# A hybrid attention and recurrence network: weight sums made by accumulating transfers in place of VectorE additions

## The chip, the cores and the metric

The kernel runs on one core of one Trainium2 chip. The time is that of the device, in microseconds, for one execution of the whole network. Before the change the median of three runs is 2181.79 us (2180.43 to 2184.33). The engines are named as the profile names them: PE (TensorE, matrix products), PEld (its weight loads), DVE (VectorE), ACT (ScalarE), POOL (GpSimd) and SP (SyncE, which here only issues transfers).

## The reference

Two layers over 1024 tokens of width 1024. Layer 0 mixes by windowed attention, layer 1 by a gated recurrence; each is followed by an MLP with a squared ReLU. All is float32.

```python
def sqrelu_mlp(h, w_up, w_down):
    return jnp.square(jax.nn.relu(h @ w_up)) @ w_down

def hgrn2_recurrence(h, lower_bound, w_in, g_norm, w_o):
    q, f, i, g = jnp.split(h @ w_in, 4, axis=-1)
    ...

def reference(...):
    for layer in range(DEPTH):
        h = rmsnorm(x, mix_norm[layer])
        if layer % N_MIXERS == 0:
            y = sliding_window_attention(h, ...)
        else:
            y = hgrn2_recurrence(h, ...)
        x = x + y
        h = rmsnorm(x, mlp_norm[layer])
        x = x + sqrelu_mlp(h, mlp_w_up[layer], mlp_w_down[layer])
    return rmsnorm(x, final_norm)
```

The change touches `h @ w_up` of both MLPs and `h @ w_in` of the recurrence.

## The kernel before

**Tiles.** Tokens stand in two halves of 512 (`hf`), features in blocks of 128. Nearly every tile is 128 x 512 float32, 256 KB. A product in full precision is made of three passes over numbers split in a high and a low part: `weight_split` (L402) casts a weight tile to `wh` (on ACT or DVE) and subtracts to get `wl` (on DVE); `split` does the same for activations into `a` tiles; `mm3` (L384) then issues high x high, high x low and low x high.

**Seven products for eight.** The first product of each MLP, and the recurrent projections, take two column blocks of weights (the `first` and the `second`), two halves of the contraction and two halves of the tokens: a 2 x 2 by 2 x 2 block product. It is made in the Winograd form of Strassen's scheme, with seven block products of 12 matmuls each (`product`, L561) in place of eight. `strassen_weights` (L567) makes the weight side: four tiles are loaded into `wr` buffers (five of them), four sums s1 to s4 are made of them on DVE into `m` buffers (seven), and the seven weights 1 to 7 are split. `finish` (L516) makes the activation side, four sums of four tiles each, at the start of each stage. `pair` (L581) is one such product of an MLP: 16 pairs a layer. `two` (L1058) is that of the recurrent projections, called twice for each of eight blocks e; the first call of each kind finds weights 1 and 2 already done by `two_first`. After the products the results are put together: ACT copies a PSUM tile out while later products add into the same tile (`main`, a `q` buffer of PSUM), DVE adds the copies.

**What sets the order.** No instruction is issued where it is written. `Schedule` (L140) records every operation with its engine, an assumed cost and the buffers it uses, and then makes one list by a simulation of its own: an operation is taken when its inputs and its buffer are free, lowest rank first. Buffers of a tag are handed out in the order of first use. Operations inside `strassen_weights` have a `lead` of 100 ranks, so weights are prepared about a pair ahead. A cast may go to ACT or DVE, whichever the plan finds free. A transfer is planned as 650 to 820 ns on SP and 2000 ns more until it has landed. On the chip each engine then takes its instructions strictly in that order and waits for semaphores. Since there are five `wh` and five `wl` buffers, a weight can be split only when the product of the weight five places earlier has ended.

**Line numbers.** Every operation is recorded through `call`, so in the trace all instructions have line L326 (before) or L328 (after); they are told apart by their tiles.

Of the kernel before, what the change touches and what calls it, by code (L numbers as in the profile page):

```python
# [22 lines left out]
TH = T // NH  # L23
FF = 4096
MT = FF // P
EPS = 1e-5
N_PAR = 8 * KT
# [13 lines left out]
BUFS = {"a": 60, "t": 18, "m": 7, "sm": 8, "wr": 5, "wh": 5, "wl": 5, "p": 4, "q": 4}  # L41
# [95 lines left out]
HK = KT // 2  # L137
# [140 lines left out]
class Net:  # L278
    def __init__(self, ctx, tc, io):
        self.nc, self.io = tc.nc, io  # L280
        self.s = Schedule()
        self.n = 0
        self.x = None
        self.pool = ctx.enter_context(tc.tile_pool(name="sb", bufs=1))
        self.pp = ctx.enter_context(tc.tile_pool(name="ps", bufs=1, space=bass.MemoryType.PSUM))
        self.dram = ctx.enter_context(tc.tile_pool(name="dr", bufs=1, space=bass.MemoryType.DRAM))
        nc = self.nc
        self.par = self.const((P, N_PAR))
        self.dma(self.par, io["par"], 4 * P * N_PAR)
# [104 lines left out]
    def gain(self, which, kt):  # L394
        return self.par[:, which * KT + kt : which * KT + kt + 1]

    def raw(self, src):
        r = self.tile("wr", BUFS["wr"], (P, TH), F32)
        self.dma(r, src, 4 * P * TH)
        return r  # L400

# [94 lines left out]
    def gained(self, which, kt, hf):  # L496

        u = self.t()
        self.act(u, self.x[kt][hf], AF.Copy, scale=self.gain(which, kt))
        return u  # L500

    def weigh(self, hf):
# [5 lines left out]
    def begin(self, which):  # L508

        self.b, self.u = {k: [] for k in range(1, 8)}, []  # L510
        for kt in range(KT):
            u = self.gained(which, kt, 0)
            self.b[1 + kt // HK].append(self.split(u))
            self.u.append(self.keep(u))

    def finish(self, which, upper_first=False):  # L516

        x, t, q01, q11 = self.b, [], [], []

        def stored(j):  # L520
            z = self.t()
            self.dma(z, self.u[j], 4 * P * TH)
            return z

        def lower():
            for j in range(HK):
                q01.append(self.gained(which, j, 1))
                t.append(stored(j))
                self.tt("any", t[j], q01[j], t[j], ALU.subtract)
                x[5].append(self.split(t[j]))  # L530

        def upper():
            for j in range(HK):
                q11.append(self.gained(which, j + HK, 1))
                x[3].append(self.split(q11[j]))

        for part in (upper, lower) if upper_first else (lower, upper):
            part()
        for j in range(HK):
            self.tt("any", t[j], q11[j], t[j], ALU.subtract)  # L540
            x[6].append(self.split(t[j]))
        for j in range(HK):
            self.tt("any", q01[j], q11[j], q01[j], ALU.subtract)
# [23 lines left out]
    def strassen_weights(self, first, second, done=()):  # L567

        self.s.lead = LEAD
        a = {(i, k): self.raw(src[:, k * TH : k * TH + TH]) for i, src in enumerate((first, second)) for k in range(2)}  # L570
        s1, s2, s3, s4 = (self.t(tag="m") for _ in range(4))
        self.tt("any", s1, a[1, 0], a[1, 1], ALU.add)
        self.tt("any", s2, s1, a[0, 0], ALU.subtract)
        self.tt("any", s3, a[0, 0], a[1, 0], ALU.subtract)
        self.tt("any", s4, a[0, 1], s2, ALU.subtract)
        order = ((1, a[0, 0]), (5, s1), (2, a[0, 1]), (6, s2), (3, s4), (7, s3), (4, a[1, 1]))
        w = {name: self.weight_split(z) for name, z in order if name not in done}
        self.s.lead = 0
        return w

# [477 lines left out]
    def two(self, which, e, x, out, begun=None):  # L1058

        w = self.strassen_weights(*(self.io["win"][i, e] for i in which), (1, 2) if begun else ())  # L1060
        main, y0 = begun or (self.psum(), self.t())
        side, own = self.psum(), begun or self.psum()
        y1, z0, z1 = (self.t() for _ in range(3))
        out += [(y0, y1), (z0, z1)]
        if not begun:
            self.product(main, w[1], x[1], True)
            self.copy(y0, main)
# [5 lines left out]
        self.copy(y1, main)  # L1073
        yield
        if not begun:
            self.product(own, w[2], x[2], True)
            self.tt("DVE", y0, own, y0, ALU.add)
# [5 lines left out]
        self.tt("DVE", y1, side, y1, ALU.add)  # L1083
        yield
        self.product(main, w[4], x[4], False)
        self.copy(z0, main)
        yield
# [287 lines left out]
```

## Time and profile before

| | before |
|---|---|
| median of 3 runs | 2181.79 us |
| span of the profiled execution, first to last instruction | 2174.9 us |
| granted clock of PE, mean over the span | 0.994 |
| DMA moved | 316.49 MB, 44.7% of the 16 engines' span |
| chain that ended last: PE, DVE, ACT, DMA | 85%, 7%, 4%, 2% |

Of the profiled execution the record has the span, and no time of its own beside it. The stages in the span: attention until about 295 us, first MLP `pair` loop 295 to 600, its second product until 935, recurrent stage 935 to 1455, its output product until 1510, second MLP 1510 to 2150, final norm at the end. A row of a group has the instruction, output and input tiles, shapes, count, then busy time and mean of one, then the idle time of the engine just ahead of such instructions and what ended it. In a row of the timeline the first number is the start in us from the span's start and the second how long it took; what stands in brackets is the idle time ahead of it and its releaser. In a row of the windows each engine has its busy time and, in parentheses, its instructions.

### The profile page before, as it was taken

The numbers are of one execution on the slowest core, as the hardware profiler recorded it, in microseconds if no ns is written. First come the engines' busy times: TensorE is split into PE (matmuls) and PEld (weight loads), VectorE is DVE, ScalarE is ACT, GpSimd is POOL, SyncE is SP. The second block draws the span as 40 slices with busy tenths as digits, with TensorE's granted clock in tenths as the row PEclk, the third lists the DMA queues.
The fourth block names the chain that finished last, engine by engine and source line by source line (L and its number), as shares of the span: only waits on it lengthen the run. The fifth ranks groups of instructions, "written<-read, shape, count | busy, mean of one in ns | idle before, by whom it ended". The sixth has DMA issues, their size and how long they took to land.

```text
span 2174.9 us, 32278 instructions
## 1 busy us (share of the span) xinstructions
PE 2129.5 (98%) x11374; PEld 1713.3 (79%) x11374; DVE 1823.6 (84%) x3608; ACT 837.7 (39%) x1757; POOL 62.4 (3%) x124
## 2 busy tenths in 40 slices
PE   8999999999999999999999999999999999999997
PEld 6777778888877887877788888878788887888786
DVE  8899889667789888899888888878976678988887
ACT  5567755122234233365333333343521223322442
POOL 4030000000000000000100000000000000000000
PEclk9999999999999999999999999999999999999999
DMA  6212363333369867741111111547333336976652
GB/s 204 75 48 83 112 194 116 105 109 111 108 204 305 274 202 234 247 136 49 56 57 59 58 53 52 188 148 227 113 114 103 107 116 224 305 241 226 209 171 78
DMA packets 174274, 316.49 MB, mean 146 GB/s; under 512 B 19616, under 2 KB 21664, under 8 KB 174112
## 3 DMA queue, kind: packets, MB, share of 16 engines
q1 hardware_dynamic: 174112, 314.43, 44.7%
q8 instruction: 89, 1.46, 0.3%
q14 instruction: 73, 0.60, 0.1%
HBM read 250.39 MB, written 63.96 MB: 145 GB/s over the span
## 4 chain that ended last, share of the span: by engine, by line
PE 85%; DVE 7%; ACT 4%; DMA 2%; issue 1%; SPq 0%; DVEq 0%; ACTq 0%
PE q L326 45%; PE p L326 40%; DVE a L326 3%; DVE t L326 2%; ACT t L326 1%; ACT a L326 1%; DVE wl L326 1%; DVE m L326 1%; DMA wr<-in_down 1%; ACT m L326 1%; ACT wh L326 0%; DMA t<-d 0%; DVE wh L326 0%; DMA d<-t 0%; DMA a<-d 0%
## 5 line engine op out<-in xcount | busy, mean ns | idle before, releaser
L326 PE MATMUL q<-a,wh 128*128 128x512 f32 x2560 | 798.6, 395 | 5.0 <-DVE t L326 2.3
L326 PE MATMUL p<-a,wh 128*128 128x512 f32 x2336 | 754.4, 402 | 9.1 <-ACT t L326 3.7
L326 PEld LDWEIGHTS q<-a,wh 128*128 128x128 f32 x2560 | 480.1, 188 | 120.5 <-ACT t L326 4.1
L326 PEld LDWEIGHTS p<-a,wh 128*128 128x128 f32 x2336 | 432.0, 189 | 107.7 <-ACT t L326 4.6
L326 PE MATMUL q<-a,wl 128*128 128x512 f32 x1280 | 499.5, 394 | 0.0
L326 PE MATMUL p<-a,wl 128*128 128x512 f32 x1168 | 462.8, 397 | 0.0
L326 PEld LDWEIGHTS q<-a,wl 128*128 128x128 f32 x1280 | 240.4, 188 | 56.6
L326 PEld LDWEIGHTS p<-a,wl 128*128 128x128 f32 x1168 | 220.4, 189 | 50.5 <-issue 0.5
L326 DVE TENSOR_TENSOR wl<-wr,wh 128x512 fp32r<-128x512 f32 x352 | 241.0, 686 | 15.5 <-ACT wh L326 5.4
L326 ACT COPY t<-q 128x512 f32<-128x512 f32 (+2 forms) x201 | 111.8, 562 | 349.0 <-PE q L326 344.1
L326 DVE TENSOR_TENSOR a<-t,a 128x512 fp32r<-128x512 f32 (+1 forms) x294 | 195.0, 685 | 0.8 <-DMA t<-d 0.5
L326 DVE CAST wh<-wr 128x512 fp32r<-128x512 f32 x204 | 87.8, 430 | 127.6 <-PE p L326 78.4
L326 DVE TENSOR_TENSOR wl<-m,wh 128x512 fp32r<-128x512 f32 x256 | 176.3, 689 | 16.1 <-ACT wh L326 6.1
L326 ACT CAST wh<-m 128x512 fp32r<-128x512 f32 x153 | 95.2, 623 | 210.4 <-PE q L326 148.4
L326 DVE TENSOR_TENSOR t<-t,t 128x512 f32<-128x512 f32 (+3 forms) x268 | 159.7, 611 | 17.7 <-DMA t<-d 10.7
L326 ACT CAST a<-t 128x512 fp32r<-128x512 f32 x189 | 114.7, 619 | 128.8 <-PE q L326 82.6
L326 ACT CAST wh<-wr 128x512 fp32r<-128x512 f32 x148 | 91.1, 619 | 172.7 <-PE p L326 109.3
L326 PE MATMUL p<-wh,a 128*128 128x512 f32 x384 | 130.6, 407 | 8.2 <-ACT a L326 7.0
L326 DVE TENSOR_TENSOR m<-wr,wr 128x512 f32<-128x512 f32 x160 | 109.7, 687 | 22.2 <-DMA wr<-in_down 11.9
L326 PEld LDWEIGHTS q<-t,t 128*64 128x64 f32 (+1 forms) x2160 | 98.0, 144 | 25.0 <-issue 11.2
L326 PE MATMUL q<-t,t 128*64 128x32 f32 (+2 forms) x2160 | 111.5, 230 | 0.0
L326 DVE CAST wh<-m 128x512 fp32r<-128x512 f32 x103 | 44.3, 430 | 73.4 <-PE q L326 59.7
(117 smaller groups left out, 2113.9 us busy)
## 6 DMA issues: line engine op xcount, KB each, us to landing
t<-d SPq DMA_DIRECT2D x296, 256.0 KB, 4.7
wr<-in_down SPq DMA_DIRECT2D x256, 256.0 KB, 3.9
d<-t SPq DMA_DIRECT2D x180, 256.0 KB, 2.4
wr<-in_up SPq DMA_DIRECT2D x128, 256.0 KB, 2.9
wr<-in_win SPq DMA_DIRECT2D x68, 256.0 KB, 2.9
a<-d SPq DMA_DIRECT2D x60, 256.0 KB, 4.4
wr<-in_wqkv SPq DMA_DIRECT2D x48, 256.0 KB, 2.8
d<-a SPq DMA_DIRECT2D x48, 256.0 KB, 2.4
```

The costliest lines, as they stand in the source:

```text
L326: fn(*[place(a) for a in args], **{k: place(v) for k, v in kw.items()})
```

## The change

The four sums of `strassen_weights` are no longer made by DVE. Two `m` tiles are loaded by SP, `rows` with A10 and `column` with A00, and further tiles are added to them in place by transfers that POOL issues with an accumulate operation (`accumulate`): `rows` becomes A10 + A11 (weight 5), then + A00 (weight 6), then + A01 (weight 3); `column` is A00 (weight 1), then + A10 (weight 7). Between two additions to a tile its split has to be done. Weights 2 and 4 are loaded by themselves. So a pair has four loads on SP as before, and four accumulating transfers besides, and uses two `m` buffers in place of four, two `wr` in place of four.

Sums with only plus signs need other signs elsewhere: the first half's activations are scaled by the negative gain (`neg_par`, one new constant), several differences in `finish` become sums or one `scalar_tensor_tensor`, `two` copies products out with a scale of -1, and in `pair` the lower half of the hidden rows, which now has the opposite sign, is squared with `min` in place of `max`. The plan assumes 1100 ns on POOL and 2500 ns more for an accumulating transfer.

```diff
+        self.neg_par = self.const((P, N_PAR))
+        self.ts("DVE", self.neg_par, self.par, -1.0, None, ALU.mult, None, N_PAR)
...
+    def accumulate(self, out, in_, nbytes):
+
+        self.op("Pool", self.nc.gpsimd.dma_start, [out], [in_, out], 1100.0, out, in_, accum_op=ALU.add, tail=2500.0)
...
-        if psum:
+        if m < MT // 2:
+            self.stt(r, c, 0.0, c, ALU.min, ALU.mult)
+        elif psum:
...
-                self.tt("any", t[j], q01[j], t[j], ALU.subtract)
+                self.tt("any", t[j], q01[j], t[j], ALU.add)
...
-            self.tt("any", t[j], q11[j], t[j], ALU.subtract)
+            self.stt(t[j], q11[j], -1.0, t[j], ALU.mult, ALU.subtract)
...
-            self.tt("any", z, z, t[j], ALU.subtract)
+            self.stt(z, z, -1.0, t[j], ALU.mult, ALU.subtract)
...
-        a = {(i, k): self.raw(src[:, k * TH : k * TH + TH]) for i, src in enumerate((first, second)) for k in range(2)}
-        s1, s2, s3, s4 = (self.t(tag="m") for _ in range(4))
-        self.tt("any", s1, a[1, 0], a[1, 1], ALU.add)
-        self.tt("any", s2, s1, a[0, 0], ALU.subtract)
-        self.tt("any", s3, a[0, 0], a[1, 0], ALU.subtract)
-        self.tt("any", s4, a[0, 1], s2, ALU.subtract)
-        order = ((1, a[0, 0]), (5, s1), (2, a[0, 1]), (6, s2), (3, s4), (7, s3), (4, a[1, 1]))
-        w = {name: self.weight_split(z) for name, z in order if name not in done}
+        a = {(i, k): src[:, k * TH : k * TH + TH] for i, src in enumerate((first, second)) for k in range(2)}
+        rows, column = self.raw(a[1, 0], "m"), self.raw(a[0, 0], "m")
+        self.accumulate(rows, a[1, 1], 4 * P * TH)
+        w = {}
+
+        def made(name, z):
+            if name not in done:
+                w[name] = self.weight_split(z)
+
+        made(1, column)
+        made(5, rows)
+        if 2 not in done:
+            made(2, self.raw(a[0, 1]))
+        self.accumulate(rows, a[0, 0], 4 * P * TH)
+        made(6, rows)
+        self.accumulate(rows, a[0, 1], 4 * P * TH)
+        made(3, rows)
+        self.accumulate(column, a[1, 0], 4 * P * TH)
+        made(7, column)
+        made(4, self.raw(a[1, 1]))
...
-        self.copy(y0, main)
+        self.act(y0, main, AF.Copy, scale=-1.0)
...
-            self.tt("DVE", y0, own, y0, ALU.add)
+            self.tt("DVE", y0, y0, own, ALU.subtract)
```

DVE's queue in the steady `pair` loop, before: from the split of weight 1 to that of weight 6, and on to the last sums. `m1164` is the tile of weight 5, `m1165` that of weight 6; the `m12..` tiles are sums for the next pair.

```order
CAST wh1170_4680<-m1164_4585 128x512
TENSOR_TENSOR wl1171_4686<-m1164_4585,wh1170_4680 128x512
TENSOR_TENSOR m1203_4692<-wr1197_4595,wr1199_4672 128x512
CAST wh1172_4700<-wr1161_4493 128x512
TENSOR_TENSOR t1150_4683<-q1146_4638,t1150_4683 128x512
TENSOR_TENSOR wl1173_4707<-wr1161_4493,wh1172_4700 128x512
SCALAR_TENSOR_TENSOR t1154_4712<-t1150_4683 128x512
CAST wh1174_4723<-m1165_4592 128x512
TENSOR_TENSOR wl1175_4730<-m1165_4592,wh1174_4723 128x512
```

The same stretch of DVE's queue now, and on to the split of weight 7; `m1244` is `rows` and `m1245` is `column`.

```order
CAST wh1248_5138<-m1244_4624 128x512
TENSOR_TENSOR wl1249_5144<-m1244_4624,wh1248_5138 128x512
CAST wh1251_5157<-wr1250_4800 128x512
TENSOR_TENSOR t1234_5141<-q1230_5096,t1234_5141 128x512
TENSOR_TENSOR wl1252_5164<-wr1250_4800,wh1251_5157 128x512
SCALAR_TENSOR_TENSOR t1238_5169<-t1234_5141 128x512
CAST wh1253_5180<-m1244_4624 128x512
TENSOR_TENSOR wl1254_5187<-m1244_4624,wh1253_5180 128x512
TENSOR_TENSOR t1233_5122<-t1233_5122,t1235_5184 128x512
SCALAR_TENSOR_TENSOR t1240_5197<-t1233_5122 128x512
SCALAR_TENSOR_TENSOR t1242_5211<-q1229_5027,t1242_5211 128x512
CAST wh1257_5222<-m1245_4773 128x512
```

The sum between the splits is gone, weights 5 and 6 are now read from one tile that is changed in between, and the cast of weight 7, which ACT had, stands on DVE. The cast of weight 3 stays on ACT, ahead of the copies out of PSUM.

POOL's queue in the same loop now (before, POOL has no instruction there): each line is an accumulating transfer, "x2" two in a row to the same tile. `m1343` is `rows` of the pair three ahead.

```order
DMA m1310_4934<-in_up 128x512
DMA m1212_4618<-in_up 128x512
DMA m1211_4469<-in_up 128x512 x2
DMA m1343_5089<-in_up 128x512
DMA m1245_4773<-in_up 128x512
DMA m1244_4624<-in_up 128x512 x2
```

For each pair POOL issues the first addition to `rows` of the pair three ahead, then the addition to this pair's `column`, then the second and third to this pair's `rows`.

DVE's queue at the start of the recurrent stage, before: `m2664` is a weight sum among the activation sums (`t`), the low parts (`a`) and the last additions of the MLP's output (`m2508`, `m2509`).

```order
TENSOR_TENSOR a2548_10005<-t2546_9778,a2547_9994 128x512
TENSOR_TENSOR m2664_10014<-wr2662_9956,wr2663_9969 128x512
TENSOR_TENSOR m2509_10018<-p1616_6833,a1531_6339 128x512
TENSOR_TENSOR t2550_9789<-t2549_10008,t2550_9789 128x512
TENSOR_TENSOR a2142_8493<-m2509_10018,a2142_8493 128x512
```

The same place now, with no sum in it.

```order
TENSOR_TENSOR a2485_9940<-t2483_9725,a2484_9929 128x512
SCALAR_TENSOR_TENSOR t2483_9725<-t2470_9686,t2483_9725 128x512
TENSOR_TENSOR m2446_9956<-p1553_6761,a1476_6284 128x512
TENSOR_TENSOR t2487_9736<-t2486_9943,t2487_9736 128x512
TENSOR_TENSOR a2079_8431<-m2446_9956,a2079_8431 128x512
```

The weight sum is gone, and one activation sum has moved forward and changed its form.

More of the change, by code (lines that the diff above doesn't have):

```diff
@@ L395, in gain, with neg_gain, raw @@
         return self.par[:, which * KT + kt : which * KT + kt + 1]
-    def raw(self, src):
-        r = self.tile("wr", BUFS["wr"], (P, TH), F32)
+    def neg_gain(self, which, kt):
+        return self.neg_par[:, which * KT + kt : which * KT + kt + 1]
+    def raw(self, src, tag="wr"):
+        r = self.tile(tag, BUFS[tag], (P, TH), F32)
         self.dma(r, src, 4 * P * TH)
@@ L494, in square_relu, with gained @@
         self.hid[m, hf] = self.keep(r)
-    def gained(self, which, kt, hf):
+    def gained(self, which, kt, hf, negative=False):
         u = self.t()
-        self.act(u, self.x[kt][hf], AF.Copy, scale=self.gain(which, kt))
+        self.act(u, self.x[kt][hf], AF.Copy, scale=(self.neg_gain if negative else self.gain)(which, kt))
         return u
@@ L511, in begin @@
         for kt in range(KT):
-            u = self.gained(which, kt, 0)
+            u = self.gained(which, kt, 0, True)
             self.b[1 + kt // HK].append(self.split(u))
@@ L533, in upper @@
             for j in range(HK):
-                q11.append(self.gained(which, j + HK, 1))
+                q11.append(self.gained(which, j + HK, 1, True))
                 x[3].append(self.split(q11[j]))
@@ L539, in finish @@
         for j in range(HK):
[L540 removed]
+            self.stt(t[j], q11[j], -1.0, t[j], ALU.mult, ALU.subtract)
             x[6].append(self.split(t[j]))
         for j in range(HK):
[L543 removed]
+            self.tt("any", q01[j], q11[j], q01[j], ALU.add)
             x[7].append(self.split(q01[j]))
@@ L1066, in two @@
             self.product(main, w[1], x[1], True)
-            self.copy(y0, main)
+            self.act(y0, main, AF.Copy, scale=-1.0)
         yield
@@ L1072, in two @@
         self.product(main, w[6], x[6], False)
-        self.copy(y1, main)
+        self.act(y1, main, AF.Copy, scale=-1.0)
         yield
@@ L1076, in two @@
             self.product(own, w[2], x[2], True)
-            self.tt("DVE", y0, own, y0, ALU.add)
+            self.tt("DVE", y0, y0, own, ALU.subtract)
         yield
@@ L1082, in two @@
         self.product(side, w[3], x[3], False)
-        self.tt("DVE", y1, side, y1, ALU.add)
+        self.tt("DVE", y1, y1, side, ALU.subtract)
         yield
```

## The prediction

> **What bounds the kernel now.** I read the page's head first, then the span cut into windows, then one stretch of the timeline engine by engine.
>
> ```profile
> span 2174.9 us, 32278 instructions
> PE 2129.5 (98%) x11374; PEld 1713.3 (79%) x11374; DVE 1823.6 (84%) x3608; ACT 837.7 (39%) x1757; POOL 62.4 (3%) x124
> ```
>
> The span is 2174.9 us; the median of the runs is 2181.79, so 6.9 us lie outside the span, and I leave those as they are. PE is idle for 2174.9 - 2129.5 = 45.4 us in all. No change that leaves the matmuls alone can win more than that and the time at a lowered clock. So the question is where these 45 us lie, and whether the weight sums are near them. The windows say so (busy us of PE, PEld, DVE, ACT, POOL with instruction counts, then granted clock, DMA share, GB/s):
>
> ```profile
> 400.00:450.00 50.00, 50.00 (x217) 40.51 (x216) 34.06 (x58) 10.27 (x18) 0.00 (x0) 1.00 0.33 106
> 450.00:500.00 50.00, 50.00 (x217) 40.54 (x216) 36.07 (x60) 10.80 (x19) 0.00 (x0) 1.00 0.34 111
> 1200.00:1250.00 50.00, 50.00 (x417) 40.50 (x416) 43.48 (x96) 19.61 (x41) 0.62 (x2) 1.00 0.18 55
> 984.00:988.00 4.00, 2.72 (x12) 1.88 (x10) 4.00 (x7) 4.00 (x9) 0.00 (x0) 1.00 0.00 0
> 988.00:992.00 4.00, 1.98 (x6) 1.28 (x7) 4.00 (x8) 3.00 (x6) 0.00 (x0) 0.85 0.00 0
> 992.00:996.00 4.00, 4.00 (x15) 3.19 (x14) 4.00 (x10) 0.59 (x1) 0.00 (x0) 0.72 0.23 66
> 1010.00:1015.00 5.00, 4.61 (x21) 3.40 (x20) 4.48 (x8) 3.67 (x7) 0.00 (x0) 1.00 0.00 0
> 1525.00:1550.00 25.00, 23.31 (x102) 18.13 (x101) 24.98 (x43) 16.82 (x32) 0.00 (x0) 1.00 0.23 76
> ```
>
> The first two rows are the first MLP's `pair` loop, the third is the recurrent projections: PE is busy for all of 50 us at full clock while DVE has 14 to 16 us free (6.5 in the third). There the sums are beside PE's work already. PE loses time only where a stage begins: at 984 to 992 (the recurrent stage), 1010 to 1015, and 1525 to 1550 (the second MLP), and there DVE is full (4.00 of 4.00, 24.98 of 25.00). So DVE time saved is worth something at those places and nothing in between.
>
> **What is removed.** The four sums of each call of `strassen_weights` (32 pairs and 16 calls of `two`, 48 calls):
>
> ```profile
> L326 DVE TENSOR_TENSOR m<-wr,wr 128x512 f32<-128x512 f32 x160 | 109.7, 687 | 22.2 <-DMA wr<-in_down 11.9 <-DMA wr<-in_up 7.9 <-DMA t<-d 1.0
> L326 DVE TENSOR_TENSOR m<-wr,m 128x512 f32<-128x512 f32 x48 | 33.0, 688 | 0.9
> L326 DVE TENSOR_TENSOR m<-m,wr 128x512 f32<-128x512 f32 x48 | 33.0, 688 | 0.9
> ```
>
> Of the 160, 64 belong to `operands` (names 5 and 7, 16 steps, two layers) and stay; 96 + 48 + 48 = 192 go, 192 x 0.688 = 132 us of DVE. The order shows that DVE also takes over casts that ACT had (the cast of weight 7 in the steady loop).
>
> What of it reaches the end, place by place. At the recurrent stage's start:
>
> ```profile
> 966.30 0.69 DVE L326 TENSOR_TENSOR t<-t,t 128x512 f32<-128x512 f32 x1 [0.72 <-ACT t L326]
> 969.31 0.69 DVE L326 TENSOR_TENSOR m<-wr,wr 128x512 f32<-128x512 f32 x1
> 969.91 0.69 DVE L326 TENSOR_TENSOR m<-p,a 128x512 f32<-128x512 f32 x1
> 1000.00 0.69 DVE L326 TENSOR_TENSOR t<-p,t 128x512 f32<-128x512 f32 x1 [0.82 <-PE p L326]
> 990.02 1.55 PE L326 MATMUL p<-a,wh 128*128 128x512 f32 x4 [3.30 <-ACT t L326]
> ```
>
> DVE runs without a pause from 966.30 to 1000.00, and PE starts again at 990.02 after 3.30 us; one sum stands in that stretch ahead of it, and an operation moves the next by 969.91 - 969.31 = 0.60 us. Gain 0.6 us. Then 0.39 us lost in 1010 to 1015, which I count as won. In 1525 to 1550 PE loses 25.00 - 23.31 = 1.69 us on a full DVE in whose queue four sums stand; four times 0.60 is more than 1.69, so I count 1.7. Together 2.7 us.
>
> **What changes its form at no cost.** A `tensor_tensor` that becomes a `scalar_tensor_tensor` in `finish`, and `min` for `max`, cost the same:
>
> ```profile
> L326 DVE TENSOR_TENSOR t<-t,t 128x512 f32<-128x512 f32 x191 | 129.0, 685 | 15.8 <-DMA t<-d 10.7 <-ACT t L326 3.4 <-DMA wr<-in_down 1.2
> L326 DVE SCALAR_TENSOR_TENSOR t<-t,t 128x512 f32<-128x512 f32 x32 | 21.8, 685 | 1.4 <-ACT t L326 1.3
> L326 ACT COPY t<-p 128x512 f32<-128x512 f32 x72 | 41.7, 583 | 54.0 <-PE p L326 53.8
> L326 ACT ACTIVATE t<-q 128x512 f32<-128x512 f32 x48 | 28.6, 595 | 25.2 <-PE q L326 19.2 <-DVE t L326 6.0
> ```
>
> 685 against 685 ns; an ACT copy with a scale 595 against 583, on an engine with 30 us of 50 free. The one new operation, `neg_par`, is 64 columns at the start, while PE waits for its first operands; I put it at nothing, and 0.2 us if it were in the way.
>
> **What is added.** 192 transfers of 256 KB, issued by POOL, each adding to a tile in place. No such transfer is in this trace, so its time L (from the last reader's end to the sum in place) is bounded by the nearest rows:
>
> ```profile
> wr<-in_up SPq DMA_DIRECT2D x128, 256.0 KB, 2.9
> d<-t SPq DMA_DIRECT2D x180, 256.0 KB, 2.4
> L326 POOL TENSOR_SCALAR a<-t 128x512 f32<-128x512 f32 x2 | 4.8, 2413 | 25.0 <-issue 18.5 <-DVE t L326 6.5
> ```
>
> Below: a plain load, 2.9 us. Above: two loads one after the other and POOL's one 128x512 operation as the issue, 2 x 2.9 + 2.4 = 8.2. I take a load and a read of the tile one after the other, 2.9 + 2.4 = 5.3, the rows nearest to what it does. POOL's own time p for one issue lies between nothing and 2.4; I take 1. DMA's share in the loop is 0.33 for eight transfers a pair; four more at twice the price make it 0.66, so the engines are not full.
>
> A tile now passes through a chain: weight 5 is split from it, A00 is added, 6 is split, A01 is added, 3 is split. The same pair in the trace, first DVE and then ACT:
>
> ```profile
> 441.87 0.43 DVE L326 CAST wh<-wr 128x512 fp32r<-128x512 f32 x1 [1.44 <-PE p L326]
> ...
> 447.96 0.69 DVE L326 TENSOR_TENSOR wl<-m,wh 128x512 fp32r<-128x512 f32 x1
> ...
> 453.00 0.43 DVE L326 CAST wh<-m 128x512 fp32r<-128x512 f32 x1 [0.55 <-PE q L326]
> 453.53 0.69 DVE L326 TENSOR_TENSOR wl<-m,wh 128x512 fp32r<-128x512 f32 x1
> ...
> 461.32 0.43 DVE L326 CAST wh<-wr 128x512 fp32r<-128x512 f32 x1 [1.43 <-PE p L326]
> ```
> ```profile
> 456.96 0.62 ACT L326 CAST wh<-m 128x512 fp32r<-128x512 f32 x1 [3.15 <-PE q L326]
> 457.49 0.59 ACT L326 ACTIVATE t<-q 128x512 f32<-128x512 f32 x1
> ```
>
> One pair lasts 461.32 - 441.87 = 19.45 us, its seven products 2.78 each. The split of 5 ends at 448.65; the cast of 6 at 453.00 waited for PE (a free `wh` buffer), not for data. So 4.35 us of L are covered. With L = 5.3 the cast of 6 comes 0.95 late (453.95), its split ends at 455.17, and the cast of 3 on ACT can start at 460.5 instead of 457.5. Behind that cast in ACT's queue stands the copy of product 1 (0.59), which product 6 waits for because it adds into the same PSUM tile. The cast at 461.32 waited for PE at the end of product 2, and product 5 ends 2.78 later, at 464.1; the copy ends at 461.7. **PE sees nothing, with 2.4 us to spare.** DVE stands for 0.95 us at the cast of 6, and has 14 us free per 50.
>
> There is a second, tighter loop. The `m` tile that the third split frees is loaded by SP for a pair three ahead, its first addition stands in POOL's queue ahead of the next pair's second addition, and POOL goes in order. Round once: L, split of 6 (1.22), L, cast and `wl` of 3 (0.62 + 0.69), load (2.9), and two more issues on POOL ahead of the next (2p; L has its own issue in it): 2(L + p) + 5.4 us. That fits in 19.45 as long as **L + p stays under 7.0**; mine is 6.3. In the recurrent stage seven products and the recurrence between them take longer than in this loop (PE's 417 instructions per 50 us against 217), so the same chain has more room, and I charge nothing there.
>
> The CAST takes 0.43 us where a subtraction of as many elements takes 0.69 in the rows above. The Trainium skill, SBUF — State Buffer, section "SBUF: two separate sides", has a rule against this change: while VectorE runs such a fast copy, GpSimd cannot write the descriptors of the transfers it issues, so that they wait. No run so far shows it. By that rule one 0.43 us cast may hold up an addition, L + p becomes 6.7, still under 7.0, and the sum is the same; without it the sum is the same too, but the margin falls from 0.7 to 0.3.
>
> **Sum.** 2181.8 - 2.7 + 0.2 = 2179.3 us. Whatever is within 0.2% (4.4 us) a measurement of this kernel can't tell from no change.
>
> **Rivals.**
> 1. *The additions are late (slower).* Place: the second loop, at POOL's queue and ACT's cast of 3. Price: over 7.0 every microsecond of L + p costs 2 us per pair, 32 pairs, 64 us. At 7.5: 2179 + 32 = 2211; at the bound 8.2 + 2.4 = 10.6: 2410. For it: the margin is 0.7 us of a quantity never seen here, and ACT and DVE go in order. Against it: both ends of the range are piled up from worst cases. Chance 0.21.
> 2. *The starts of stages recover altogether (faster).* If the gap of 3.30 at 990 vanished, the lowered clock behind it would too (0.15 x 4 + 0.28 x 4 = 1.7 us); with 1.69 and 0.39 that makes 7.1, and 2174.7. For it: DVE is full there. Against it: what PE waits for at 990 is an ACT copy behind casts that the order leaves in place. Chance 0.17.
> 3. *DVE instructions of every kind hold back POOL's issues.* After the split of 6, three to four 0.60 us operations stand back to back on DVE: 2.4 us more, L + p = 8.7, 2 x 1.7 x 32 = 109 us, 2288. Chance 0.03.
>
> **How the numbers follow.** No visible change 0.59, its own range 2177.5 to 2183; faster 0.17; slower 0.24. The range 2173 to 2202 takes in the forecast, the second rival, and the first up to L + p = 7.3; it leaves out some 0.16, nearly all above.
>
> **What would show it.** Right: windows of 50.00 in both loops, DVE's busy time down by some 110 us (132 less the casts it takes over), L between 4 and 6 in the issue table, the gap at 990 shorter by about 0.6, the loss at 1525 to 1550 gone. Wrong: PE gaps in the `pair` loop released by ACT `t` or by `wh`, once per pair, with ACT or DVE waiting for the additions; or a lowered clock in the loops.

## The result, and the profile after

The changed kernel takes **2213.57 us** (median of four runs, 2199.36 to 2224.38) against 2181.11 us for the kernel before (four runs beside them): a ratio of **1.0142, 95% interval 1.0100 to 1.0183**, so 32 us slower. The forecast was 2179.3 us, the range ended at 2202. The changed kernel also varies more: its four runs lie 25 us apart, those of the kernel before 4 us. The profiled run is the fastest of the four (2199.36 us, of which 1.8 lie outside the span). Two executions below ran at a lowered clock throughout and are left out of the times: e5's profiled one (2332.35 us, mean clock 0.848) and one of e3's (2990.93 us, 0.654).

The head of the page of the changed kernel, and its two large queues (packets, MB, share of 16 engines):

```profile
span 2197.6 us, 32688 instructions
...
PE 2135.2 (97%) x11374; PEld 1710.3 (78%) x11374; DVE 1725.9 (79%) x3473; ACT 806.5 (37%) x1703; POOL 229.2 (10%) x316
...
q1 hardware_dynamic: 173824, 313.91, 43.7%
q0 software_dynamic: 27648, 50.34, 15.1%
```

DVE lost 98 us, as the change intends (forecast: some 110). PE's idle time grew from 45.4 to 62.4 us, and PE is busy 5.7 us longer with as many instructions. The mean granted clock isn't lower (0.995 against 0.994), so a slower clock over the span doesn't account for that; what does stays open. The accumulating transfers are the whole of q0.

The windows that answer to those of before (busy us of PE, PEld, DVE, ACT, POOL with counts; granted clock, DMA share, GB/s):

```profile
400.00:450.00 50.00, 49.77 (x215) 40.00 (x214) 30.41 (x55) 9.40 (x17) 8.31 (x10) 1.00 0.65 161
450.00:500.00 50.00, 50.00 (x217) 40.53 (x216) 28.08 (x51) 8.46 (x15) 10.19 (x12) 1.00 0.69 158
1200.00:1250.00 50.00, 50.00 (x431) 40.14 (x430) 40.76 (x96) 16.19 (x36) 6.65 (x9) 1.00 0.45 95
1000.00:1004.00 4.00, 3.92 (x11) 3.07 (x12) 4.00 (x9) 0.55 (x2) 0.86 (x1) 0.59 0.31 31
1525.00:1550.00 25.00, 24.63 (x107) 19.56 (x106) 25.00 (x43) 18.58 (x34) 1.72 (x2) 1.00 0.51 147
```

In this run the loops hold, or nearly: PE 50.00 of 50 between 450 and 500, DMA share 0.69 where 0.66 was forecast. The stages begin as before: DVE is full behind 1000 us (4.00 of 4.00), where the recurrent part starts, and the clock is lowered after the gap there. Most of the loss is somewhere else, at the hand-over from the `pair` loop to the MLP's second product (`down`); the products of the last pair reach to about 640 us, beyond the 600 that the list of stages gives for the loop. Four stretches of 10 us there, the first two of the kernel before, the last two of the changed one:

```profile
630.00:640.00 10.00, 10.00 (x45) 8.14 (x44) 9.90 (x18) 5.83 (x10) 0.00 (x0) 1.00 0.94 301
640.00:650.00 10.00, 10.00 (x45) 8.08 (x44) 9.01 (x16) 5.99 (x12) 0.00 (x0) 1.00 0.88 280
```
```profile
630.00:640.00 10.00, 10.00 (x45) 8.15 (x44) 4.47 (x9) 1.16 (x3) 1.27 (x2) 1.00 0.64 183
640.00:650.00 10.00, 6.69 (x29) 4.82 (x27) 7.75 (x14) 5.75 (x12) 0.00 (x0) 1.00 0.97 310
```

Before, DVE (9.90 of 10), ACT (5.83) and the transfer engines (0.94) prepare `down` from 630 us on, while PE still works on the last pair. After, DVE has 4.47 and ACT 1.16 in those ten microseconds, and the same preparation comes some 7 us later, when PE already needs it. The timeline says what holds it. First the kernel before, DVE:

```profile
629.93 0.43 DVE L326 CAST wh<-m 128x512 fp32r<-128x512 f32 x1 [0.55 <-PE q L326]
...
632.88 0.69 DVE L326 TENSOR_TENSOR m<-wr,wr 128x512 f32<-128x512 f32 x1
```

and the changed kernel, POOL, DVE, POOL, ACT and PE in turn, in order of time:

```profile
629.55 0.86 POOL L328 DMA_DIRECT2D m<-in_up  x1 [2.43 <-DVE wl L328]
636.91 0.43 DVE L328 CAST wh<-m 128x512 fp32r<-128x512 f32 x1 [5.42 <-PE q L328]
638.43 0.86 POOL L328 DMA_DIRECT2D m<-in_up  x1 [8.02 <-DVE wl L328]
639.86 0.69 DVE L328 TENSOR_TENSOR m<-wr,wr 128x512 f32<-128x512 f32 x1
644.28 1.14 ACT L328 CAST wh<-m 128x512 fp32r<-128x512 f32 x2 [3.73 <-DMA m<-in_up]
645.33 0.58 ACT L328 COPY t<-q 128x512 f32<-128x512 f32 x1
645.96 0.73 PE L328 MATMUL q<-a,wh 128*128 128x512 f32 x2 [2.64 <-ACT t L328]
666.79 0.74 PE L328 MATMUL q<-a,wh 128*128 128x512 f32 x2 [2.38 <-DVE t L328]
```

`m<-wr,wr` is a sum of `down`'s own weights. In both kernels it stands in DVE's queue behind a cast from the last pair's row sum (weight 6). That cast runs at 629.93 before and at 636.91 after, and takes everything behind it along. Its row names PE as what ended the wait, but the sum that it reads, issued at 629.55, was there only then. Here is its row in the table of issues (of 629.4 to 629.7 us; the last number is the time from issue to landing), and the window from the issue to the cast:

```profile
m<-in_up POOLq DMA_DIRECT2D x1, 256.0 KB, 7.3
```
```profile
629.55:636.91 7.36, 7.36 (x34) 5.98 (x33) 1.94 (x5) 0.59 (x1) 0.86 (x1) 1.00 0.89 244
```

629.55 + 7.3 is 636.85, and the cast starts within 0.1 us of that. So the cast waits for the transfer, which takes 7.3 us where the median of all pairs is 4.8 (below), while the transfer engines are busy 0.89 of the time. The next sum can be issued only when weight 6 is split, at 638.43, and the cast from it starts at 644.28, 5.85 us later, while `down`'s loads are under way too (the engines are at 0.97 from 640 to 650). ACT stands 3.73 us at that cast, with a second cast and the copy that PE waits for right behind it. PE's gaps from 640 to 670 us add up to 7.29 us (five of them, the first and the last shown; 0.84 before). Further on the reloads come late too: PE loses 2.31 us at 844 (0.29 before), and the second MLP's hand-over gives 0.73 + 1.40 + 2.19 us from 1852 to 1866 (1.44 before).

The accumulating transfers themselves, by issue to landing, and a plain load beside them:

```profile
m<-in_up POOLq DMA_DIRECT2D x128, 256.0 KB, 4.8
...
wr<-in_up SPq DMA_DIRECT2D x64, 256.0 KB, 3.5
...
m<-in_win POOLq DMA_DIRECT2D x64, 256.0 KB, 4.1
```

Two theories fit this so far. **A/D: waiting.** A sum that passes through three transfers, each behind the split of the weight before, is late, and the casts from it hold up what stands behind them in the queues of ACT and DVE (A: because the transfers land late; D: because the plan takes them for 3.6 us and so places other work behind the casts). **B: traffic.** The 50 MB more delay the other loads, whether or not anybody waits for a sum. A third, **C**, puts it on the moved signs.

### The profile page after: what moved, and what is told of

It reads as the page before. It is cut to its first block, busy times and chain, and to the rows that moved or that the text cites. A ratio compares the mean times of both kernels' runs of the same rounds, so it can differ in the third digit from the quotient of the medians.

```text
span 2197.6 us, 32688 instructions
## 1 busy us (share of the span) xinstructions
PE 2135.2 (97%) x11374; PEld 1710.3 (78%) x11374; DVE 1725.9 (79%) x3473; ACT 806.5 (37%) x1703; POOL 229.2 (10%) x316
## 2 busy tenths in 40 slices
DMA packets 201638, 366.34 MB, mean 167 GB/s; under 512 B 22656, under 2 KB 24704, under 8 KB 201472
## 3 DMA queue, kind: packets, MB, share of 16 engines
q0 software_dynamic: 27648, 50.34, 15.1%
## 4 chain that ended last, share of the span: by engine, by line
PE 77%; DVE 8%; DMA 7%; ACT 4%; issue 3%; SPq 1%; DVEq 0%; ACTq 0%; POOLq 0%
PE q L328 42%; PE p L328 35%; DMA wr<-in_down 3%; DVE a L328 3%; DVE t L328 3%; ACT a L328 2%; ACT t L328 2%; DVE wl L328 1%; DVE m L328 1%; DMA t<-d 1%; DMA d<-t 1%; DMA m<-in_up 1%; ACT m L328 1%; ACT wh L328 1%; SPq L328 1%
## 5 line engine op out<-in xcount | busy, mean ns | idle before, releaser
L328 DVE TENSOR_TENSOR wl<-m,wh 128x512 fp32r<-128x512 f32 x302 | 205.9, 690 | 73.5 <-ACT wh L328 59.8
L328 DVE TENSOR_TENSOR wl<-wr,wh 128x512 fp32r<-128x512 f32 x306 | 209.6, 687 | 8.4 <-ACT wh L328 1.0
L328 DVE CAST wh<-m 128x512 fp32r<-128x512 f32 x186 | 79.3, 426 | 151.7 <-DMA m<-in_up 72.5
L328 POOL DMA_DIRECT2D m<-in_up x128 | 112.6, 963 | 682.2 <-DVE wl L328 458.2
L328 DVE TENSOR_TENSOR t<-t,t 128x512 f32<-128x512 f32 (+2 forms) x244 | 144.4, 605 | 16.5 <-DMA t<-d 11.0
L328 DVE CAST wh<-wr 128x512 fp32r<-128x512 f32 x182 | 78.2, 430 | 99.7 <-PE q L328 52.3
L328 ACT CAST wh<-m 128x512 fp32r<-128x512 f32 x116 | 71.4, 618 | 162.8 <-DMA m<-in_up 79.0
L328 POOL DMA_DIRECT2D m<-in_win x64 | 55.6, 873 | 655.7 <-ACT a L328 318.7
L328 ACT CAST a<-a 128x512 fp32r<-128x512 f32 x113 | 69.7, 622 | 138.6 <-DVE a L328 69.3
L328 ACT CAST wh<-wr 128x512 fp32r<-128x512 f32 x124 | 76.2, 618 | 112.6 <-PE p L328 72.0
```

What stands on the lines that cost most here:

```text
L328: fn(*[place(a) for a in args], **{k: place(v) for k, v in kw.items()})
```

## The experiments

Each ratio is to the kernel before, run on the same chip beside it (medians 2180.8 to 2181.5 us).

**The changed kernel once more (e1).** No edit.

> The changed kernel unchanged, as a control and for a second profile. Every theory expects about 2210 us and a spread of some 20 us between runs; a profile of a longer run than the first (span 2197.6) should show by which gaps of PE the runs differ: theory A (accumulates land late where the pair loop hands over to the MLP's second product) expects the extra gaps right behind 640 and 830 us and behind 1850 us, with releaser ACT t or ACT wh, and a lowered clock after each gap of over 3 us.

Measured: 2214.81 us, ratio 1.0149 (1.0130 to 1.0167). This profile has a span of 2213.6 us, 16.0 more than the first. The hand-overs are a little worse (3.85 us at 654 and 2.59 at 675 are the largest gaps of the first MLP's). But it also has what nobody expected of it: gaps in the middle of the `pair` loop, 0.57 to 1.14 us in six pairs between 486 and 609 us, and three of 0.90 to 1.94 from 1757 to 1800, 9.1 us together. PE's busy time is 6.7 us longer (2141.9 against 2135.2), at a mean granted clock of 0.990 against 0.995. One such pair, POOL, DVE, POOL, ACT, PE:

```profile
511.14 2.75 POOL L328 DMA_DIRECT2D m<-in_up  x3 [8.82 <-DVE wl L328]
520.26 0.43 DVE L328 CAST wh<-m 128x512 fp32r<-128x512 f32 x1 [5.55 <-DMA m<-in_up]
521.78 0.86 POOL L328 DMA_DIRECT2D m<-in_up  x1 [7.89 <-DVE wl L328]
526.53 0.62 ACT L328 CAST wh<-m 128x512 fp32r<-128x512 f32 x1 [6.52 <-DMA m<-in_up]
527.68 0.72 PE L328 MATMUL q<-a,wh 128*128 128x512 f32 x2 [1.14 <-ACT t L328]
```

and the same instructions in the first profile, where PE has no gap:

```profile
508.26 2.65 POOL L328 DMA_DIRECT2D m<-in_up  x3 [9.04 <-DVE wl L328]
516.00 0.43 DVE L328 CAST wh<-m 128x512 fp32r<-128x512 f32 x1 [3.04 <-DMA m<-in_up]
517.52 0.86 POOL L328 DMA_DIRECT2D m<-in_up  x1 [6.62 <-DVE wl L328]
521.41 0.62 ACT L328 CAST wh<-m 128x512 fp32r<-128x512 f32 x1 [3.17 <-DMA m<-in_up]
```

POOL issues three transfers in a row: two that are wanted later (a first sum several pairs ahead and a column sum) and, third, A00 for this pair, which DVE waits for. From the first issue to the cast it is 7.74 us in the one profile and 9.12 in the other; for the single one after it (A01) 3.89 and 4.75. With the 0.3 us from a split's end to the issue (521.48 to 521.78) the two together make 12.2 and 14.5 us, **6.1 and 7.2 us per addition, on either side of the 7.0** that the prediction worked out as the point where the loop no longer fits. So the prediction's first rival is real, and the kernel sits at its edge. Between these two profiles that makes 9.1 of the 16.0 us.

**The sums back on DVE, the signs kept (e2).** This separates C (the call in `two` is changed likewise).

```diff
-        w = self.strassen_weights(*(self.io["up"][self.layer, i] for i in (m, m + MT // 2)))
+        w = self.strassen_sums(*(self.io["up"][self.layer, i] for i in (m, m + MT // 2)))
...
+        s1, s2, s3, s4 = (self.t(tag="m") for _ in range(4))
+        self.tt("any", s1, a[1, 0], a[1, 1], ALU.add)
+        self.tt("any", s2, s1, a[0, 0], ALU.add)
+        self.tt("any", s3, a[0, 0], a[1, 0], ALU.add)
+        self.tt("any", s4, a[0, 1], s2, ALU.add)
```

> All four sums of every pair and every 'two' are made by VectorE again, from five loads, with the moved signs kept (plain sums, negated gains, scale -1 evictions). Theories A (late accumulates) and B (extra transfer traffic) expect the time of before, 2178 to 2184 us, POOL without DMA issues and PE 2129 to 2130 us busy. Theory C (the moved signs or the new forms on ACT and DVE cost) expects 2190 us or more.

Measured: 2182.02 us, 1.0003 (0.9992 to 1.0013), PE busy 2132.0 us, 2 us above what was expected. C falls: the signs and new forms cost nothing that can be measured, as the prediction said.

**The last two pairs of each MLP on DVE (e3), and a longer planned time (e4).**

```diff
+        make = self.strassen_sums if m >= MT // 2 - 2 else self.strassen_weights
```
```diff
-        self.op("Pool", self.nc.gpsimd.dma_start, [out], [in_, out], 1100.0, out, in_, accum_op=ALU.add, tail=2500.0)
+        self.op("Pool", self.nc.gpsimd.dma_start, [out], [in_, out], 1100.0, out, in_, accum_op=ALU.add, tail=4700.0)
```

> Only the last two pairs of each of the two MLPs (4 of 48 units of four sums) get their sums from VectorE; all others by accumulating transfers. Theory A expects the junction behind the pair loop to lose its gaps (7.3 us of PE idle from 645 to 667 us in the changed kernel, and about 4 us behind 1850 us): 2193 to 2200 us. Theory B in the form that all the added traffic delays loads everywhere expects one twelfth of the loss back, 2208 to 2212 us. Theory C expects no change, 2210 to 2215 us.

> The planner's assumed time of an accumulating transfer goes from 1.1 + 2.5 us to 1.1 + 4.7 us, near the 4.8 and 4.1 us to landing that the trace shows; nothing else is changed. Theory D (the order is wrong because the plan takes the sum to be there 1.2 to 2.2 us too early, so ACT and DVE stand at casts with other work behind) expects most of the loss back, 2185 to 2195 us. Theory A in the form that the transfers are late only where down's loads fill the DMA engines (landing 5.8 us) expects a part, 2195 to 2205 us. Theory B expects no change, 2207 to 2215 us.

Measured: e3 2194.91 us, 1.0063 (1.0050 to 1.0076): with 4 of 48 units changed, 19 of the 32 us come back, as A expects. Of the 14 us that are left, its profile has 4.9 as gaps of 0.42 to 1.76 us in six pairs between 448 and 552 us, and 2.3 in three pairs from 1629 to 1671: the loop's edge again. e4 **2186.86 us, 1.0025 (1.0014 to 1.0037)**: with nothing but the order changed and every transfer still there, 27 of the 32 us come back, as D expects. What ACT and DVE waited for transfers into `m` (total us, times, longest) in the first profile of the changed kernel and in e4:

```profile
ACT wh L328 <- DMA m<-in_up: 79.0, 29, 5.6
...
DVE wh L328 <- DMA m<-in_up: 72.5, 30, 5.3
```
```profile
ACT wh L328 <- DMA m<-in_up: 63.2, 42, 6.1
...
DVE wh L328 <- DMA m<-in_up: 9.5, 9, 2.9
```

In the slower profile e1 the same two rows have 125.7 and 132.3 us. In e4 no gap of PE of 0.25 us or more is left inside either `pair` loop; at the hand-overs one of 2.45 us remains at 656 us, and 0.79 and 2.14 at 1838 and 1847. At the first hand-over the second and third addition of the last pair take 5.5 and 6.4 us from issue to landing (7.3 and 5.8 in the changed kernel). The last one is no faster, but ACT now has eight instructions, most of them casts, from 636 to 642 us ahead of the cast that waits for it (the changed kernel has two, from 639 to 641), and PE has no gap between 630 and 650:

```profile
643.25 0.62 ACT L328 CAST wh<-m 128x512 fp32r<-128x512 f32 x1 [1.20 <-DMA m<-in_up]
```

ACT waits 1.20 us there in place of 3.73. So late landings cost little where the order has put other work ahead of the casts.

**Traffic without waits (e5, e12; e14).** Sums on DVE; behind the last use of each sum an accumulating transfer (in e14 a plain load, on the same POOL queue) writes into its dead buffer.

```diff
+        for z, (i, k) in ((s1, (1, 1)), (s2, (0, 0)), (s4, (0, 1)), (s3, (1, 0))):
+            self.accumulate(z, (first, second)[i][:, k * TH : k * TH + TH], 4 * P * TH)
```

> VectorE makes the sums, as in the kernel with VectorE's sums; behind the last use of each sum, an accumulating transfer adds a quarter of the weights to that sum's buffer, which nobody reads any more. So the transfers and GpSimd's issues are there (192, in their places, plus 192 loads that the changed kernel saves: DMA traffic is above the changed kernel's), but no cast waits for one. Theory B (the added traffic delays other loads) expects the loss of the changed kernel or more, 2200 to 2215 us, with gaps of PE at the hand-over from the pair loop to the second product. Theories A and D (casts in the in-order queues of ACT and DVE stand for late sums) expect at most 4 us over the kernel before, 2180 to 2185 us.

> The kernel with VectorE's sums and accumulating transfers that nobody waits for, once more, for a profile at the usual clock: 2186 to 2192 us. If its 8 us over the kernel before come from full transfer engines, its extra gaps of PE stand at the hand-overs (640 to 670 us, 830 to 850 us, 1840 to 1870 us) and wait for down's loads; if they come from GpSimd's issues or longer VectorE instructions, they are spread over the loops.

> As the kernel with accumulates that nobody waits for (2190 to 2192 us), but the same 192 transfers of 256 KB on GpSimd's queue are plain loads into the dead buffers. If bytes and issues are the price, the same time, 2188 to 2193 us. If it is the longer work of an accumulating transfer on the 16 engines (1.73 us against 0.80 us in the queues' shares), about half of the 9 to 11 us stays, 2184 to 2187 us.

One remark on e5's expectation: it says that the traffic is above the changed kernel's, and that is wrong. The changed kernel loads eight tiles per unit as this one does; 366.86 against 366.34 MB. Measured: e5 2190.10 us, 1.0034 (1.0020 to 1.0047); e12 repeats it for a profile: 2192.39 us, 1.0052 (1.0033 to 1.0070, two runs). e14: 2185.78 us, 1.0026 (1.0014 to 1.0038). Of the 32 us some 9 to 11 come without any wait for a sum. A and D had said at most 4 and miss here; B had said 19 or more and misses too. In e12 the loops are whole and the loss is at the hand-overs, where PE (second column) and the clock (column behind POOL) suffer; the queue rows are e12's and then e14's:

```profile
450.00:500.00 50.00, 50.00 (x217) 40.55 (x216) 36.53 (x62) 10.45 (x20) 9.26 (x11) 1.00 0.67 159
640.00:670.00 30.00, 27.27 (x110) 21.34 (x109) 26.87 (x46) 15.53 (x28) 1.05 (x2) 0.94 0.94 309
1850.00:1880.00 30.00, 27.34 (x111) 21.75 (x110) 27.91 (x46) 13.65 (x24) 0.00 (x0) 0.94 0.90 292
```
```profile
q0 software_dynamic: 27648, 50.34, 15.1%
```
```profile
q0 software_dynamic: 15360, 50.34, 7.9%
```

e12 does have a wait of its own: what is written next into a dead buffer has to wait until the transfer into it has landed. In the recurrent part DVE waits 12.5 us so (16 times, the longest 2.0 us, at 1309), and PE has one gap there that the kernel before doesn't have, 1.05 us at 1314. So the 9 to 11 us needn't be traffic alone.

An accumulating transfer takes 15.1% x 2190.4 / 192 = 1.72 us of all 16 engines, a plain load of the same bytes 7.9% x 2183.1 / 192 = 0.90. The median with plain loads is lower too, but its interval overlaps that of e5, and barely that of e12's two runs as well, so that a difference in time isn't clear.

**Only the recurrent projections (e6), only the pairs (e7).** Each keeps `strassen_weights` at one of its two calls.

> Accumulating transfers only in the recurrent projections (64 of the 192); the pairs of the MLPs get their sums from VectorE. Theories A and D expect the one gap of 0.35 to 0.39 us in each of six units that the changed kernel shows there, and the first start at 1000 us unhelped: 2181 to 2186 us. Theory B expects a third of the loss, 2190 us or more.

> Accumulating transfers only in the pairs of the MLPs (128 of the 192); the recurrent projections get their sums from VectorE. Theories A and D expect nearly the whole loss, 2204 to 2214 us, with the spread of the changed kernel (15 us or more between runs). Theory B expects two thirds, about 2203 us.

Measured: e6 2184.83 us, 1.0010 (1.0000 to 1.0020), with the six gaps of 0.35 to 0.37 us that were expected; e7 2203.42 us, 1.0099 (1.0085 to 1.0113), with a spread of 3 us and not the 15 expected, and no gap in the loops of its profile. So 22 us are the pairs' alone, and the recurrent part is nearly free; that the two together cost more than their sum of 25 us isn't explained by these runs.

**Which two of the four sums (e10, e13).** The cleanest test: the same 96 accumulates, either the two that depend on no earlier split, issued ahead, or the two on the chain; DVE makes the others. The planned time is the changed kernel's. First e10, then e13:

```diff
+        self.accumulate(rows, a[1, 1], 4 * P * TH)
+        self.accumulate(column, a[1, 0], 4 * P * TH)
...
+        self.tt("any", rows, rows, corner, ALU.add)
+        made(6, rows)
+        self.tt("any", rows, rows, other, ALU.add)
```
```diff
+        self.tt("any", rows, a[1, 0], a[1, 1], ALU.add)
+        self.tt("any", column, a[0, 0], a[1, 0], ALU.add)
...
+        self.accumulate(rows, first[:, :TH], 4 * P * TH)
+        made(6, rows)
+        self.accumulate(rows, first[:, TH:], 4 * P * TH)
```

> Two of the four sums of each unit accumulate (the first, A10 + A11, and the column sum, both issued ahead and with no earlier sum to wait for); the two on the chain (A00 and A01 added to the row sum) are VectorE additions from loads. Planned time of an accumulate as in the changed kernel. If the loss is that the chain of three accumulates (5, 6, 3) is late and holds the queues of ACT and DVE, this gives 2178 to 2185 us with no gap of PE in the pair loops. If any accumulate costs by its traffic or its issue, about half the loss stays, 2192 us or more.

> The counterpart of the kernel with the two accumulates off the chain: VectorE makes A10 + A11 and the column sum; the two sums on the chain (A00, then A01, added to the row sum behind the casts of weights 5 and 6) accumulate. As many accumulates (96), and one plain load fewer. If the chain is what costs, 2190 to 2205 us, with casts on ACT or DVE that wait for transfers into m and gaps of PE from 640 to 670 us. If any accumulate costs alike, the time is that of the off-chain kernel, 2177 to 2182 us.

Measured: e10, off the chain, **2178.99 us, 0.9988 (0.9979 to 0.9996)**; e13, on the chain, **2201.27 us, 1.0094 (1.0079 to 1.0109)**. The same number of accumulates, 22 us apart: with this planned time it is their place in the chain that costs. (On the chain there is one plain load fewer per unit, so more traffic can't be the reason.) Off the chain, ACT and DVE never wait for a transfer into `m` from the MLP's weights, and POOL does the waiting. The windows of e10 and then of e13:

```profile
640.00:670.00 30.00, 29.01 (x125) 23.21 (x125) 28.87 (x49) 16.10 (x29) 0.00 (x0) 1.00 0.91 303
```
```profile
450.00:500.00 50.00, 50.00 (x217) 40.49 (x216) 32.08 (x56) 8.76 (x16) 4.98 (x6) 1.00 0.54 138
640.00:670.00 30.00, 25.37 (x100) 19.16 (x99) 26.69 (x44) 16.56 (x31) 0.00 (x0) 0.94 0.89 294
1850.00:1880.00 30.00, 25.60 (x98) 19.66 (x96) 25.93 (x43) 13.12 (x25) 0.00 (x0) 0.89 0.84 270
```

e13 loses 4.6 and 4.4 us of PE at the two hand-overs, with a granted clock of 0.94 and 0.89 in these windows (in its first profile the changed kernel lost 7.3 and 4.3), and has no gap in the loops, where POOL has no other issues ahead of A00. So under the short planned time the chain by itself makes the hand-over late. It isn't all of the 22 us: of the 11.2 us by which PE's idle time differs between these two profiles, some 8 lie at the hand-overs and some 5 in the recurrent part, while other places gain a little.

**Versions that combine (e8, e9, e11, e15).** e8 is e3 and e4 together; e9 is e8 with the recurrent sums on DVE; e11 is e4 with a tail of 6200; e15 is e10 with the tail of 4700.

> The longer planned time of an accumulating transfer (1.1 + 4.7 us), and the sums of the last two pairs of each MLP made by VectorE. If what is left of the loss with the longer plan alone (6 us) is the hand-over (a gap of 2.45 us at 656 us with a lowered clock behind it, and 2.1 us at 1847 us), this gives 2180 to 2183 us. If it is the recurrent part and the starts, it gives 2185 to 2187 us.

> As the kernel with the longer planned time and the last two pairs on VectorE (2177.7 us), and the recurrent projections' sums on VectorE as well. The recurrent part's six gaps of 0.37 us (2.2 us together) should go: 2174 to 2177 us. If VectorE's 44 us more there cost something else, or the accumulates there paid for themselves elsewhere, 2178 us or more.

> All sums accumulate; the planner takes an accumulating transfer as 1.1 + 6.2 us (the changed kernel 1.1 + 2.5, the longer plan 1.1 + 4.7). If what the longer plan left at the hand-over (gap of 2.45 us at 656 us) is still lateness of the sums, 2178 to 2183 us. If it is the transfer engines being full there (share 0.93 from 640 to 660 us), so that down's loads and the reloads of spilled tiles come late whatever the plan says, 2184 to 2190 us.

> Two accumulates off the chain as in the kernel of 2179.0 us, with the longer planned time (1.1 + 4.7 us). With no cast waiting for a late sum there, the plan should matter little: 2176 to 2181 us by the theory that only the chain's lateness costs. If the longer plan is a gain by itself (another order of all engines), 2170 to 2176 us.

| run | median us | ratio (95% interval) |
|---|---|---|
| e8, longer plan, last two pairs on DVE | 2177.73 | 0.9984 (0.9975 to 0.9992) |
| e9, as e8, recurrent sums on DVE | 2178.78 | 0.9992 (0.9983 to 1.0001) |
| e11, plan of 7.3 us | 2191.37 | 1.0044 (1.0030 to 1.0058) |
| e15, off the chain, longer plan | 2179.17 | 0.9985 (0.9975 to 0.9994) |

e8, e10 and e15 are below the kernel before by 0.12 to 0.16%: their intervals lie under 1, but the difference is within the 0.2% that was set as the limit of what can be told. e9 misses its 2174 to 2177: the six gaps go and nothing is gained. e11 is above all that was expected: a plan that allows still more for a transfer does worse (2.28 us lost at 661, 2.82 at 1861), so "allow more time" is no rule, and why this order is worse was not followed up. Here the window in which the prediction had seen a gain of 1.7 us, in e8:

```profile
1525.00:1550.00 25.00, 25.00 (x110) 20.22 (x109) 25.00 (x43) 17.90 (x33) 3.87 (x5) 1.00 0.59 151
```

## Why the prediction was wrong

- **What bounds the kernel** held: PE, with its idle time at the places where stages meet, and DVE time in the loops worth nothing.
- **The gain of 2.7 us** came only in small part. At the recurrent start the gap is 3.24 us where it was 3.30, in place of the 0.6 less: DVE is as full there without the sum. The 0.39 us behind it, counted as won, became 0.69 and 1.70 (at 1005 and 1019 us). In 1525 to 1550 the changed kernel still loses 0.37 us, and 1.00 us just behind it, where 0.87 + 0.27 + 0.54 were lost before. In the kernel before the four sums stand in DVE's queue from 1542 to 1546, behind the first two of these gaps (1535 and 1536), so taking them out could by itself reach only the 0.54. With the longer plan (e8) the window is whole, so the 1.7 us could be won, by another order.
- **Form and signs at no cost**: right (e2).
- **The size of an addition**: 5.3 us was taken, 4.8 from issue to landing measured in the pairs, 4.1 in the recurrent part; the issue 0.86 us where 1 was taken. The Trainium skill, SBUF — State Buffer, section "SBUF: two separate sides", has a fast DVE copy hold back POOL's descriptor writing. The prediction put that at 0.43 us per addition; the margin is 0.3 with it and 0.7 without, where its sentence reads the other way round. The median issue here is the shortest one or 3 ns more (862 and 865 ns), the longest 1756, the mean 963 in the pairs: at most 0.10 us of POOL's own time for an issue on the average can be put down to that rule. What it may add between issue and landing no run separates.

```profile
L328 POOL DMA_DIRECT2D m<-in_up x128: 862/865/1756, 262.0 to 1838.4; - x128
```

- **The tighter loop, L + p under 7.0**: the mechanism and the limit were right, and the margin was mis-sized. L was taken as one number. A00, third of three issues in a row, takes 7.7 or 9.1 us from the first of them to the cast, and A01 alone 3.9 or 4.8; together 6.1 or 7.2 per addition in two profiles of one kernel. That was rival 1, with a chance of 0.21 and 2211 us at 7.5. (In the working of the chain the cast of 3 stands at 456.96 in the row, not at 457.5; nothing hangs on it.)
- **The step that failed** is the length L of an addition at the end of the loop: "I take a load and a read of the tile one after the other, 2.9 + 2.4 = 5.3", backed by "four more at twice the price make it 0.66, so the engines are not full", and with it the sum, in which only the loops and the starts of stages have a term. In the loop the share did become 0.69. But the last pair has the next stage's preparation beside it in the transfer engines and behind it in the queues of DVE and ACT. There the engines were at 0.94 already in the kernel before; in the changed kernel A00 takes 7.3 us from issue to landing and A01 5.8, the cast of weight 6 runs 7 us later than before, and `down`'s preparation, which stands behind it in both kernels, 7 us later too. The 4.35 us of cover and the "nothing" for PE were numbers of the steady loop. The hand-overs cost 7.3 us of PE at the first and 4.3 at the second in the first profile (0.84 and 1.44 before); e3 has 19 us back from four units, and e13 against e10 differ by 22 us, some 8 of 11 us of idle PE at the hand-overs. The prediction named the rows that would show it (gaps released by ACT `t`, ACT waiting for additions) and looked for them in the `pair` loop.
- **The recurrent stage charged nothing**: nearly right. Six gaps of some 0.37 us stand there, 2.2 us, of which the kernel before has the like of one (0.35 at 1410), and the 0.69 and 1.70 us at its start; e6, which has them all, is at 1.0010.

Of the 32 us, then: 9 to 11 come with traffic and issues that nobody waits for (e5, e12), most at the hand-overs; the rest with the waits and the order that the chain makes (e13, e4). The parts aren't additive: with the better order of e4 all the traffic is there, and only 6 us are lost. What remains open is why one execution of the changed kernel slips over the edge in its loops and another doesn't, and how e4's gain divides between the order at the hand-overs and that in the loops. The chain off and on (e10, e13) was compared under the short planned time alone.

## What to carry to other kernels

Before work is moved from an engine to transfers, follow one value through all of its transfers: additions that can be issued far ahead were free here, and a chain in which each waits for a use of the one before cost 22 us with no more traffic, as long as the plan took a transfer for 3.6 us. Cover worked out in a steady loop says nothing of its last round: look at what stands in the queues behind the last iteration, and how full the transfer engines already are there. Where a plan written in the kernel sets the order, a new operation's assumed time is part of the change; here that one number was worth 27 of 32 us, and a larger correction was worth less.

## What the runs showed of the hardware

- An accumulating transfer of 256 KB from DRAM into SBUF costs 1.72 us of the 16 engines against 0.90 for a plain load on the same POOL queue, 1.9 times as much (e12, e14), in 144 packets against 80. The Trainium skill, Collectives: The Full Stack, section "The bandwidth ceiling: the fold count and why AG ≠ RS ≠ AR", says of collectives that ReduceScatter runs at half the rate of AllGather because its add needs two source reads; the measured ratio agrees, in another use.
- POOL's own time for issuing it is 862 ns, and 538 ns for the plain load (e14).
- From issue to landing 4.8 us (median, pairs) against 3.4 for the plain loads on POOL's queue in e14. At the end of the loop, with the transfer engines busy 0.89 of the time, one took 7.3. From the first of three issues in a row to the cast that reads the third it was 7.7 and 9.1 us.
- Four runs of the changed kernel lie 25 us apart, six of e4, with the same instructions in another order, 5 us.
